# An RWKV-7 scan on one core: the output's store moved two thirds into the next period, a fourth buffer of V, and the second half's token tiles fetched one by one

## The chip, the cores and the metric

One core of a Trainium2 chip runs the whole program. The metric is the device time of one execution in microseconds (us). Three runs of the kernel before gave 2653.22, 2655.47 and 2659.98 us; the median, 2655.47 us, is the number that the change is compared with. A fourth execution was profiled, and all rows below come from it.

## What is computed

The reference is a trunk of two layers on 1024 tokens of width 1024, in float32. The change lies in the second layer's mixer, RWKV-7 time mixing. Cut to what matters here:

```
r, k, v = projections of x;  w = decay(x);  a, g = gates(x)
kk = normalize(k * k_k);  k = k * (1 + (a - 1) * k_a)
per head of 64, over the tokens t in order:
    S = S * w_t + (S @ -kk_t) (kk_t * a_t)^T + v_t k_t^T
    y_t = S @ r_t
y = group_norm(y) * ln_g + ln_b + sum(r * k * r_k) * v
mix = (y * g) @ w_out                     # the output projection
x = LN(alpha * x + mix)                   # then the feed-forward block
```

## The kernel before

**The stages.** Layer 0 and its feed-forward block come first, then phase C (the projections of layer 1, written to scratch tensors in DRAM), phase D (the scan), phase E (the output projection with its layer norm) and the last feed-forward block. The change touches D and E.

**The scan (`phase_d`).** The scan works in 32 units: 16 chunks of 64 tokens times 2 groups of 8 heads. A unit passes through five generators: `cumulate` (E), `decay` (D), `scores` (P), `inverse` (I) and `chain` (C). One turn of the loop is called a period. In period i the chain of unit i runs beside the inverse of unit i+1, the scores of unit i+2, the decay of unit i+3 and the cumulated sum of unit i+4; the string `ORDER` says in which turn the generators take their steps. Tokens flow through the chain alone (C): it computes `z`, `p1`, `r1`, `py`, `UV`, `pS` and at last the output y, which TensorE leaves in `py` and which GpSimd (POOL) then normalizes, gains, adds to and gates in six operations (L1415, L1419 to L1421, L1424, L1431). Only after L1431 is y ready to be stored.

**The loads and stores of the scan.** All of them are issued on the queue of SyncE (SP), which works in order: an entry that waits for a semaphore holds every entry behind it. A period has 13 issues: two stores of y (L1446, the two halves of `store`), two loads each of V into `V` (L1236) and into `UV` (L1235), one each of SW and KN (L1219), four of K and KA (L1223) and one of R (L1225). Buffers are rings: `y` has 2, `V` 3, `R` 3, `UV` 4, and the tiles that take SW with KN and K with KA come from a pool of 8, which is four units' worth. V's buffer is free again once POOL has run L1423 (`bo`, the bonus) of the unit that held it; the tile of SW and KN is free once VectorE (DVE) has run L1271 of `decay`.

**What sets the order.** The program's text gives priorities, and a planner at build time puts every instruction into its engine's queue: among those that it takes to be ready by its own estimate, the earliest in the text comes first. So loads and early steps of later units run ahead of their place in the text, as far as the rings let them. `pace` adds an edge that the planner alone sees: the instruction gets its place in the queue not before the last matmul traced so far has its own; at run time it waits for nothing more. Before the change, `store(us[i - 1])` is the first thing in the text of period i, ahead of the loads, and it is not paced.

**The output projection (`phase_e`).** The 1024 tokens are 8 tiles (tt). For each tile `get_y` loads 128 rows of y (L1514 through L177, one of three `wraw` buffers) and the residual (L1518), lets POOL apply gain and bias to the residual (`ln_gain`, L355 and L356), turns y round on TensorE (L1525) and splits it into two parts on ScalarE (ACT) and DVE (L200, L203). `mmh(tt, n)` is a half of the projection: 24 matmuls (L232 to L234) against the weights `units[n]`, four tiles each of `w_o[n]`, which `load_unit` loads (L177, also `wraw`) and splits (L192 on ACT, L193 on DVE). `ln(tt)` is the layer norm with its reciprocal root on POOL (L272), its scaling on ACT (L279) and its transposes on TensorE (L298). Tiles 0 and 1 are done inside the end of the scan (`early`). Then the text has: the four loads of `w_o[1]`; tiles 2 and 3 (`get_y`, first half); `get_y` of tiles 4 to 7 in one go; the second half of tiles 0 to 3 with their layer norms; then the second half and after it the first half of tiles 4 to 7 with theirs.

Of the kernel before, what the change touches and what calls it, by code (L numbers as in the profile page):

```python
# [58 lines left out]
def f(ap):  # L59
    return ap.bitcast(F32)  # L60
# [13 lines left out]
AHEAD = 4  # L74
INV = 1

ORDER = "ICIPCEIPDICPIECDICPICICPDICI"
SCAN_EARLY = 32


E_EARLY, E_LOAD, E_TURN, E_PER, E_LN = 2, (175, 153, 140, 29), 33, 1, 1
# [66 lines left out]
def big(c, name, dtype=F32, cols=1024):  # L148

    t = c.pool.tile([P, SLOT * 4 // mybir.dt.size(dtype)], dtype, name=name, tag="big", bufs=N_ARENA)  # L150
    return t[:, 0:cols]


def tmp(c, name, dtype=F32):
    return c.pool.tile([P, 512], dtype, name=name, tag="t", bufs=N_T)
# [19 lines left out]
def raw_load(c, src, n=1024):  # L175
    raw = c.pool.tile([P, 1024], F32, name="wraw", tag="wraw", bufs=N_RAW)
    d = c.nc.sync.dma_start(raw[:, 0:n], src)  # L177
    if c.first_loads:
        after(c, d, c.first_loads)
    return raw  # L180


def load_unit(c, src, arena=False, lo_eng=None):

    nc = c.nc
    raw = raw_load(c, src)
    if arena:
        hi, lo = big(c, "whi", F32R), big(c, "wlo", F32R)
    else:
        hi = c.pool.tile([P, 1024], F32R, name="whi", tag="w", bufs=N_W)  # L190
        lo = c.pool.tile([P, 1024], F32R, name="wlo", tag="w", bufs=N_W)
    nc.scalar.copy(hi, raw)  # L192
    (lo_eng or nc.vector).tensor_tensor(lo, raw, f(hi), op=ALU.subtract)  # L193
    return hi, lo
# [11 lines left out]
def pace(c, ins):  # L206

    return after(c, ins, c.last_mm)


def after(c, ins, dep):

    c.tc.add_manual_dep(ins.ins, dep.ins.name, mybir.DependencyInfo(
        mybir.DependencyClass.NoSync, mybir.DependencyReason.SCHED_ONLY), reason="pace")
    return ins
# [932 lines left out]
def phase_d(c, scr, scrv, scry, l_g2):  # L1148
# [10 lines left out]
    nc, tc, sc = c.nc, c.tc, c.scan  # L1159
    NG = NH // 2 // HP  # L1160
    W = HP * CH
# [4 lines left out]
    half = [slice(0, 64), slice(64, 128)]  # L1166
# [3 lines left out]
    def rings(plan, n, dtype=F32):  # L1170
        pool, at = Ring(c, plan[0][0], n, sum(k for _, k in plan), dtype).bufs, 0
        for name, k in plan:
            r = Ring.__new__(Ring)
            r.bufs, r.i = pool[at:at + k], 0
            at += k
            R1[name] = r
    rings([("ra", INV + 3), ("bk", 2), ("bktm", NA), ("UV", INV + 3), ("AT", 2 * NA)], 2 * W)
    rings([("R", 3), ("cl", 2), ("Em", 2), ("rk", 2), ("S", 2 * NG), ("dS", 2), ("u1", 2), ("y", 2),
           ("V", 3), ("gg", 2), ("bo", 2)], W)
    rings([("E", 4)], HP * (CH + 2))  # L1180
    rings([("TT", 2)], HP * P, F32R)
    rings([("zr", 3)], W, F32R)
# [3 lines left out]
    for i, t_ in enumerate(R1["AT"].bufs):  # L1186
        e = 1 - i % 2
# [5 lines left out]
    S = [None] * NG  # L1193
# [241 lines left out]
    seq = [(ch, g) for ch in range(T // CH) for g in range(NG)]  # L1435
    us = {}
# [5 lines left out]
    def store(u):  # L1442
        dst = scry[u.ch * CH:(u.ch + 1) * CH, u.g * 2 * W:(u.g + 1) * 2 * W].rearrange(
            "t (k e j) -> t e k j", k=HP, e=2)
        for e in range(2):
            nc.sync.dma_start(dst[:, e], u.y[half[e]])  # L1446

    def by_half(name):

# [11 lines left out]
    through(decay(us[0]))  # L1461
    for i in range(-INV - 1, len(seq)):
        gens = {}
        if i > 0:
            store(us[i - 1])
        if i + AHEAD + 1 < len(seq):
            load(i + AHEAD + 1, *seq[i + AHEAD + 1])
        if 0 <= i + INV + 1 < len(seq):
            load_v(us[i + INV + 1])
        if i + AHEAD < len(seq):  # L1470
            gens["E"] = cumulate(us[i + AHEAD])
        if i + INV + 2 < len(seq):
            gens["D"] = decay(us[i + INV + 2])
        if i >= 0:
            gens["C"] = chain(us[i], us.get(i + NG))
        if 0 <= i + INV < len(seq):
            gens["I"] = inverse(us[i + INV])
        if i + INV + 1 < len(seq):
            gens["P"] = scores(us[i + INV + 1])
        if i == 0:  # L1480
            g2 = c.pool.tile([P, 1024], F32, name="g2", tag="w", bufs=N_W)
            nc.sync.dma_start(g2, l_g2)
            g2 = g2.rearrange("p (g k e j) -> p g e k j", g=NG, k=HP, e=2)
            lg, lb = by_half("rln_g"), by_half("rln_b")
        for s in ORDER:
            if s in gens:
                fresh[0] = True
                next(gens[s], None)
                if s in "CIP":
                    yield  # L1490
        for gen in gens.values():
            assert next(gen, "end") == "end"
    store(us[len(seq) - 1])

def phase_e(c, scry, xres, w_o, scan, res):

    nc = c.nc  # L1500
    acc, xc, ys, st = [None] * 8, Seven(), [None] * 8, [None] * 8

    def last_unit():

        raw, r = raw_load(c, w_o[0, 3]), ([], [])
        for e in range(2):
            src = raw[:, e * 512:(e + 1) * 512]
            for lst, nm in zip(r, ("hi", "lo")):
                lst.append(tmp(c, "wq" + nm, F32R))
            split(c, r[0][e], r[1][e], src)  # L1510
        return r

    def get_y(tt, b):
        y = raw_load(c, scry[tt * P:(tt + 1) * P, :])  # L1514
        yh = big(c, "yh", F32R).rearrange("p (k t) -> p k t", k=KT)
        yl = big(c, "yl", F32R).rearrange("p (k t) -> p k t", k=KT)
        acc[tt] = big(c, "acc")
        nc.sync.dma_start(acc[tt], xres[tt * P:(tt + 1) * P, :])  # L1518
        ln_gain(c, acc[tt], rows_)
        st[tt] = norm_stats(c, D)  # L1520
        for q in range(2):
            pt = bank(c, b, "pt", [P, 4, P])
            for j in range(4):
                k = q * 4 + j
                c.last_mm = nc.tensor.transpose(pt[:, j, :], y[:, k * P:(k + 1) * P], c.ident)  # L1525
            split(c, yh[:, q * 4:q * 4 + 4, :], yl[:, q * 4:q * 4 + 4, :], pt)
            yield
        ys[tt] = yh, yl

    def mmh(tt, n, b):  # L1530
        p = bank(c, b, "po")
        for k in range(KT):
            mm3(c, p, ys[tt], units[n][k // 2], k == 0, k == KT - 1, lambda y_: y_[:, k, :],
                lambda w: w[k % 2] if isinstance(w, list) else w[:, (k % 2) * 512:(k % 2) * 512 + 512])
            yield
        an = acc[tt][:, n * 512:(n + 1) * 512]
        nc.vector.scalar_tensor_tensor(an, an, ALPHA, p, op0=ALU.mult, op1=ALU.add)
        nc.vector.bn_stats(st[tt][:, n, :], an)

    def ln(tt):  # L1540
        ln_to_T(c, acc[tt], tt, "mix1", xc, res, st=st[tt])

    def early():
        for tt in range(E_EARLY):
            if tt == 0:
                yield from get_y(tt, "c")
            if tt + 1 < E_EARLY:
                yield from get_y(tt + 1, "c")
            yield from mmh(tt, 0, "c")

    def through(gen):
        for _ in gen:
            pass
    total = 32 * sum(ORDER.count(s) for s in "CIP") - SCAN_EARLY
    rows_ = [big(c, "g_row"), c.pool.tile([P, 1024], F32, name="b_row", tag="w", bufs=N_W)]
    for r, n in zip(rows_, ("ffn0_g", "ffn0_b")):
        nc.sync.dma_start(r, c.row(n).to_broadcast([P, D]))
    units, first, i = [[], []], early(), 0
    for i in range(total):
        next(scan)  # L1560
        left = total - 1 - i
        for q in range(4):
            if left == E_LOAD[q]:
                units[0].append(load_unit(c, w_o[0, q]) if q < 3 else last_unit())
        if left < E_TURN:
            for _ in range(E_PER):
                next(first, None)
    assert next(scan, "end") == "end"
    through(first)
    units[0][3] = load_unit(c, w_o[0, 3])  # L1570
    units[1] = [load_unit(c, w_o[1, q], arena=True) for q in range(4)]
    done = E_EARLY
    for h in range(2):
        for tt in range(4 * h, 4 * h + 4):
            if ys[tt] is None:
                through(get_y(tt, "b"))
            if tt >= done:
                through(mmh(tt, h, "a"))
        if h == 0:
            for tt in range(4, 8):  # L1580
                through(get_y(tt, "b"))
        for tt in range(4 * h, 4 * h + 4):
            through(mmh(tt, 1 - h, "a"))
            if tt % 4 >= E_LN:
                ln(tt - E_LN)
        for tt in range(4 * h + 4 - E_LN, 4 * h + 4):
            ln(tt)
    return xc


# [77 lines left out]
```

## Time and profile before

| | |
|---|---|
| median of 3 runs | 2655.47 us (2653.22 to 2659.98) |
| the profiled execution: time | 2657.45 us |
| the profiled execution: span from first to last instruction | 2655.7 us |
| mean granted TensorE clock | 0.971 |
| TensorE (PE) busy | 2517.7 us, 95% |
| DVE, ACT, POOL busy | 1697.4, 1136.5, 517.8 us |

The span is 1.75 us shorter than the execution's own time, and that time is 1.98 us over the median. Busy shares are means over stages of different kinds. The scan's periods lie between 1380 and 1860 us of the span, the rest of phase E up to about 1952 us. In the rows, PE is TensorE's matmuls, a trailing q marks an engine's queue, and the granted clock is a share of the full 2.4 GHz; the chip grants either 1.2 or 2.4 GHz, so a mean between 0.5 and 1.0 is a mixture of both.

### The profile page before, as it was taken

What the parts mean: (1) busy time and instruction counts of PE and PEld (TensorE: products, weight loads), DVE (VectorE), ACT (ScalarE), POOL (GpSimd) and SP (SyncE); (2) the same over time, 40 slices, a digit from 0 to 9 for tenths busy, and PEclk for the clock granted to TensorE, in tenths of its full rate; (3) what the DMA queues carried; (4) which work ended last, traced back from release to release, by engine and by line L of the source; (5) the groups of instructions that cost most, each with busy time, mean ns of one, the idle gap of its engine ahead of it and who ended that gap; (6) DMA issues with size and microseconds to landing.
All of it is one profiled execution on the core that took longest, in us unless ns stands there. A gap on an engine that the chain in (4) does not pass through costs nothing.

```text
span 2655.7 us, 41419 instructions
## 1 busy us (share of the span) xinstructions
PE 2517.7 (95%) x16064; PEld 2004.7 (75%) x16064; DVE 1697.4 (64%) x2981; ACT 1136.5 (43%) x2192; POOL 517.8 (19%) x526
## 2 busy tenths in 40 slices
PE   8999999999999999999998878788899999999997
PEld 6677868888878786777777767676677888878785
DVE  7775596666648428777846667675477666657534
ACT  3115552323323327777746666674352333322230
POOL 0012250000007000010214555465300000006003
PEclk9999999999999999999998789899899999999999
DMA  3403322222235433555764333322223222225451
GB/s 145 125 20 109 115 84 88 87 80 80 81 126 198 150 124 107 163 157 165 207 164 101 91 89 86 76 52 96 105 88 103 80 87 74 86 99 188 146 169 64
DMA packets 257605, 295.79 MB, mean 111 GB/s; under 512 B 149888, under 2 KB 190976, under 8 KB 257408
## 3 DMA queue, kind: packets, MB, share of 16 engines
q1 hardware_dynamic: 256256, 291.05, 35.3%
q8 instruction: 126, 2.06, 0.3%
q10 hardware_dynamic: 1152, 2.10, 0.2%
q14 instruction: 71, 0.58, 0.1%
HBM read 219.56 MB, written 69.21 MB: 109 GB/s over the span
## 4 chain that ended last, share of the span: by engine, by line
PE 65%; DVE 9%; issue 9%; DMA 7%; POOL 6%; ACT 4%; SPq 1%; DVEq 0%; ACTq 0%; POOLq 0%
PE py L646 14%; PE pz L646 9%; PE px L646 8%; DMA wraw<-in_f_out_dram 2%; PE pv L232 2%; PE pd L232 1%; PE pd L233 1%; PE pd L234 1%; PE po L232 1%; PE po L233 1%; PE po L234 1%; PE pv L233 1%; POOL acc L355 1%; PE pv L234 1%; PE pA L1204 1%
## 5 line engine op out<-in xcount | busy, mean ns | idle before, releaser
L646 PE MATMUL py<-xch,wb 128*128 128x512 f32 x1056 | 356.5, 400 | 2.9 <-DVE u L695 2.1
L200 ACT CAST wb<-wraw 128x512 fp32r<-128x512 f32 x220 | 135.6, 619 | 398.6 <-PE py L646 177.4
L232 PE MATMUL pd<-wb,hh 128*128 128x512 f32 x704 | 277.5, 394 | 5.1 <-DVE acc L735 5.0
L234 PE MATMUL pd<-wb,hl 128*128 128x512 f32 x704 | 278.0, 395 | 0.0
L233 PE MATMUL pd<-wb,hh 128*128 128x512 f32 x704 | 277.7, 394 | 0.0
L646 PEld LDWEIGHTS py<-xch,wb 128*128 128x128 f32 x1056 | 199.7, 189 | 61.4 <-DVE u L695 15.3
L203 DVE TENSOR_TENSOR wb<-wraw,wb 128x512 fp32r<-128x512 f32 x220 | 171.8, 784 | 112.9 <-ACT wb L200 110.6
L355 POOL TENSOR_TENSOR acc<-acc,g_row 128x1024 f32<-128x1024 f32 x24 | 65.8, 2743 | 897.6 <-DMA acc<-res 880.3
L646 PE MATMUL px<-xch,wb 128*128 128x512 f32 x704 | 234.4, 396 | 3.3 <-ACT p L657 3.3
L646 PE MATMUL pz<-xch,wb 128*128 128x512 f32 x704 | 233.1, 392 | 4.5 <-ACT xch L200 4.5
L200 ACT CAST wb<-sums 128x512 fp32r<-128x512 f32 x176 | 108.8, 622 | 256.7 <-PE pz L646 145.2
L646 PE MATMUL py<-xcl,wb 128*128 128x512 f32 x528 | 209.0, 396 | 1.6 <-DVE xcl L203 1.6
L203 DVE TENSOR_TENSOR wb<-sums,wb 128x512 fp32r<-128x512 f32 x176 | 123.0, 702 | 102.6 <-ACT wb L200 101.7
L203 DVE TENSOR_TENSOR hl<-wraw,hh 128x1024 fp32r<-128x1024 f32 x72 | 126.9, 1771 | 89.5 <-ACT hh L200 89.4
L1204 PEld LDWEIGHTS <-lt 128*128 128x128 f16 x1792 | 88.0, 102 | 103.2 <-issue 77.7
L232 PEld LDWEIGHTS pd<-wb,hh 128*128 128x128 f32 x704 | 133.1, 189 | 37.3 <-issue 4.4
L646 PEld LDWEIGHTS px<-xch,wb 128*128 128x128 f32 x704 | 132.7, 189 | 35.2 <-ACT p L657 5.5
L646 PEld LDWEIGHTS pz<-xch,wb 128*128 128x128 f32 x704 | 132.0, 188 | 35.0 <-ACT xch L200 5.3
L1204 PE MATMUL pX<-lt 128*128 128x64 f16 x1280 | 92.2, 201 | 69.2 <-DVE lt L1337 38.8
L233 PEld LDWEIGHTS pd<-wb,hh 128*128 128x128 f32 x704 | 132.7, 189 | 30.0
L234 PEld LDWEIGHTS pd<-wb,hl 128*128 128x128 f32 x704 | 132.7, 189 | 29.7
L193 DVE TENSOR_TENSOR wlo<-wraw,whi 128x1024 fp32r<-128x1024 f32 x82 | 103.0, 1262 | 69.9 <-ACT whi L192 46.8
(313 smaller groups left out, 5706.6 us busy)
## 6 DMA issues: line engine op xcount, KB each, us to landing
wraw<-in_f_in_dram SPq DMA_DIRECT2D x96, 512.0 KB, 3.6
wraw<-scr_h SPq DMA_DIRECT2D x72, 512.0 KB, 3.9
scr_h<-hf SPq DMA_DIRECT2D x44, 512.0 KB, 2.6
wraw<-in_f_out_dram SPq DMA_DIRECT2D x88, 256.0 KB, 2.7
res<-acc SPq DMA_DIRECT2D x16, 512.0 KB, 2.6
acc<-res SPq DMA_DIRECT2D x16, 512.0 KB, 4.2
wraw<-in_w_r_dram SPq DMA_DIRECT2D x16, 512.0 KB, 4.0
wraw<-in_w_k_dram SPq DMA_DIRECT2D x16, 512.0 KB, 4.2
```

The costliest lines, as they stand in the source:

```text
L193: (lo_eng or nc.vector).tensor_tensor(lo, raw, f(hi), op=ALU.subtract)
L200: nc.scalar.copy(hi, src)
L203: return (eng or nc.vector).tensor_tensor(lo, src, f(hi), op=ALU.subtract)
L232: nc.tensor.matmul(ps, ls(ah), rs(bh), start=start, stop=False)
L233: nc.tensor.matmul(ps, ls(ah), rs(bl), start=False, stop=False)
L234: c.last_mm = nc.tensor.matmul(ps, ls(al), rs(bh), start=False, stop=stop)
L355: c.nc.gpsimd.tensor_tensor(x, x, rows[0], op=ALU.mult)
L646: c.last_mm = nc.tensor.matmul(ps, a_[:, k * P:(k + 1) * P], b_[:, k % 2, :], start=start and k == i == 0, stop=False, skip_group_check=True)
L1204: keep(nc.tensor.matmul(*a, **k))
```

## The change

In the scan the store becomes a generator of its own, Y. `ORDER` gets one Y after its twentieth letter, between the fifth and the sixth step of the chain, and both halves of the store are paced there. `store` of unit i-1 so stands in the text of period i behind its loads and behind two thirds of its steps. The ring of y grows from 2 to 3 and that of V from 3 to 4; together the rings of that size were 26 and become 28 pieces of 256 columns, four to a slot, so they still fill seven slots. In phase E the loads of `w_o[1]` come in pairs behind tile 2 and tile 3, `get_y` of tile tt+4 comes right behind the second half of tile tt, and the first half of tiles 4 to 7 comes before their second half.

```diff
-ORDER = "ICIPCEIPDICPIECDICPICICPDICI"
+ORDER = "ICIPCEIPDICPIECDICPIYCICPDICI"
...
-    rings([... ("u1", 2), ("y", 2),
-           ("V", 3), ("gg", 2), ("bo", 2)], W)
+    rings([... ("u1", 2), ("y", 3),
+           ("V", 4), ("gg", 2), ("bo", 2)], W)
...
         for e in range(2):
-            nc.sync.dma_start(dst[:, e], u.y[half[e]])
+            pace(c, nc.sync.dma_start(dst[:, e], u.y[half[e]]))
+        yield
...
     for i in range(-INV - 1, len(seq)):
         gens = {}
-        if i > 0:
-            store(us[i - 1])
...
             gens["P"] = scores(us[i + INV + 1])
+        if i > 0:
+            gens["Y"] = store(us[i - 1])
...
-    store(us[len(seq) - 1])
+    through(store(us[len(seq) - 1]))
...
     units[0][3] = load_unit(c, w_o[0, 3])
-    units[1] = [load_unit(c, w_o[1, q], arena=True) for q in range(4)]
-    done = E_EARLY
+    for tt in range(E_EARLY, 4):
+        through(get_y(tt, "b"))
+        through(mmh(tt, 0, "a"))
+        for q in range(2 * tt - 4, 2 * tt - 2):
+            units[1].append(load_unit(c, w_o[1, q], arena=True))
     for h in range(2):
         for tt in range(4 * h, 4 * h + 4):
-            if ys[tt] is None:
-                through(get_y(tt, "b"))
-            if tt >= done:
-                through(mmh(tt, h, "a"))
-        if h == 0:
-            for tt in range(4, 8):
-                through(get_y(tt, "b"))
-        for tt in range(4 * h, 4 * h + 4):
-            through(mmh(tt, 1 - h, "a"))
+            through(mmh(tt, 1, "a"))
+            if h == 0:
+
+                through(get_y(tt + 4, "b"))
             if tt % 4 >= E_LN:
                 ln(tt - E_LN)
         for tt in range(4 * h + 4 - E_LN, 4 * h + 4):
             ln(tt)
+        if h == 0:
+            for tt in range(4, 8):
+                through(mmh(tt, 0, "a"))
```

## Rows read from the trace of the kernel before

**Rows 1.** The page's head: span and instructions.

```profile
span 2655.7 us, 41419 instructions
```

**Rows 2.** Windows by stage: stretch, its length, busy us (instructions), clock, DMA.

```profile
core 0: us, PE busy (x) PEld busy (x) DVE busy (x) ACT busy (x) POOL busy (x), PEclk, DMA share, GB/s
1421.80:1740.30 318.50, 263.92 (x4490) 225.65 (x4487) 217.83 (x641) 203.18 (x600) 170.47 (x222) 0.87 0.38 87
1800.20:1860.00 59.80, 51.69 (x543) 40.31 (x541) 29.99 (x69) 23.58 (x56) 36.97 (x32) 0.91 0.33 106
1860.00:1952.00 92.00, 80.43 (x371) 65.22 (x369) 40.85 (x90) 29.64 (x52) 23.58 (x15) 0.93 0.25 96
```

**Rows 3.** The same stretch with line L1369 alone, one instruction in each period.

```profile
1421.80:1740.30 318.50, 8.26 (x22) 0.87 0.38 87
1740.30:1800.20 59.90, 1.88 (x5) 1.00 0.18 43
```

**Rows 4.** Waits of the SP queue, 1421.8 to 1740.3: us, times, longest us.

```profile
SPq L1446 <- POOL R L1423: 92.2, 21, 6.7
```

**Rows 5.** Waits of the engines, 1421.8 to 1740.3: us, times, longest us.

```profile
PE pX L1204 <- DVE lt L1337: 36.1, 38, 5.4
DVE R L1242 <- DMA ld<-scr_SW: 29.3, 14, 4.0
...
DVE dv L1255 <- POOL R L1400: 2.6, 1, 2.6
DVE wlo L193 <- ACT whi L192: 2.5, 3, 1.1
```

**Rows 6.** Timeline of the SP queue, periods 19 and 20: start, us, issue.

```profile
1665.83 0.37 SPq L1219 DMA_DIRECT2D ld<-scr_SW  x1
...
1683.08 1.25 SPq L1446 DMA_DIRECT2D scr_y<-R  x2
1684.44 1.25 SPq L1236 DMA_DIRECT2D R<-scr_v  x2
1686.11 0.37 SPq L1219 DMA_DIRECT2D ld<-scr_SW  x1
```

**Rows 7.** Timeline of DVE, then of POOL, in the same two periods.

```profile
1671.36 1.21 DVE L1242 TENSOR_TENSOR_SCAN R<-rst,ld 128x256 f32<-128x256 f32 x1
...
1677.84 0.42 DVE L1271 TENSOR_TENSOR ra<-ld,E 128x256 f32<-128x256 f32 x1 [0.37 <-PE pz L1204]
...
1690.05 0.69 DVE L1242 TENSOR_TENSOR_SCAN R<-rst,ld 128x256 f32<-128x256 f32 x1 [4.01 <-DMA ld<-scr_SW]
...
1683.01 0.61 POOL L1423 TENSOR_TENSOR R<-R,bon 128x256 f32<-128x256 f32 x1
```

**Rows 8.** Windows of single periods, 19 to 22 and 24, columns as in Rows 2.

```profile
1666.00:1678.80 12.80, 11.44 (x213) 9.69 (x210) 9.65 (x29) 8.45 (x28) 6.71 (x10) 0.96 0.34 77
1678.80:1695.50 16.70, 11.85 (x204) 9.90 (x201) 9.79 (x29) 9.81 (x28) 8.03 (x12) 0.87 0.31 70
1695.50:1711.60 16.10, 15.43 (x215) 13.46 (x212) 10.04 (x29) 8.59 (x27) 6.74 (x10) 0.61 0.28 63
1711.60:1727.50 15.90, 11.77 (x204) 9.84 (x199) 9.86 (x29) 9.75 (x28) 7.96 (x12) 0.82 0.33 73
...
1740.30:1752.30 12.00, 10.51 (x210) 8.95 (x208) 9.43 (x28) 9.27 (x26) 7.08 (x11) 1.00 0.23 51
```

**Rows 9.** Timelines at the scan's end: SP, ACT, PE and POOL.

```profile
1824.89 1.25 SPq L1446 DMA_DIRECT2D scr_y<-R  x2
...
1830.44 1.04 ACT L192 CAST whi<-wraw 128x1024 fp32r<-128x1024 f32 x1 [9.79 <-DMA wraw<-in_w_o_dram]
...
1832.08 0.37 PE L1204 MATMUL pX<-lt 128*128 128x64 f16 x4 [6.16 <-ACT lt L1328]
...
1816.74 3.39 POOL L355 TENSOR_TENSOR acc<-acc,g_row 128x1024 f32<-128x1024 f32 x1
```

**Rows 10.** Timeline of PE in phase E after the scan, its two longest waits.

```profile
1867.37 1.06 PE L1525 MATMUL pt<-ident,wraw 128*128 128x128 f32 x8 [2.22 <-DMA wraw<-scr_y]
...
1886.61 1.97 PE L298 MATMUL pt<-ident,acc 128*128 128x128 f32 x8 [7.81 <-ACT acc L279]
```

More of the change, by code (lines that the diff above doesn't have):

```diff
@@ L1177, in phase_d @@
     rings([("ra", INV + 3), ("bk", 2), ("bktm", NA), ("UV", INV + 3), ("AT", 2 * NA)], 2 * W)
-    rings([("R", 3), ("cl", 2), ("Em", 2), ("rk", 2), ("S", 2 * NG), ("dS", 2), ("u1", 2), ("y", 2),
-           ("V", 3), ("gg", 2), ("bo", 2)], W)
+    rings([("R", 3), ("cl", 2), ("Em", 2), ("rk", 2), ("S", 2 * NG), ("dS", 2), ("u1", 2), ("y", 3),
+           ("V", 4), ("gg", 2), ("bo", 2)], W)
     rings([("E", 4)], HP * (CH + 2))
```

## The prediction

> **What bounds the kernel now.** The page's head gives the span [rows 1]; the change reaches two stretches of it, so I read those by windows first. The scan's middle, 22 periods from 1421.8 us on, takes 318.5 us [rows 2, 3]: 14.48 us a period. TensorE is busy in only 263.9 of them, and its granted clock is 0.87 on the mean, so part of the time runs at the 1.2 GHz level. The five periods behind it, where the last loads have been issued, take 59.9 us at 1.00 [rows 3]: 12.0 each, with the same chain, inverse and scores. So 2.5 us of each earlier period are no work of TensorE's.
>
> The list of waits says what they are. VectorE stood 29.3 us, 14 times, before L1242, the cumulated sum of a later unit, until that unit's SW had landed [rows 5]. VectorE is in order, so the masked copies of the inverse (L1337) queue behind it, and TensorE in its turn waits 36.1 us for L1337 [rows 5]. The queue of SP says why SW is late: the store stood 92.2 us in 21 waits for POOL [rows 4]. The row names L1423, but L1423 starts as L1431 ends, so this is y's own last operation.
>
> Two neighbouring periods show both cases. In period 19 SW is issued at 1665.83, ahead of the store, and its sum runs at 1671.36 with no wait [rows 6, 7]; the period takes 12.8 us at 0.96 [rows 8]. In period 20 SW's tile is free when L1271 ends, at 1677.84 + 0.42 = 1678.26; but SP stands at the store until 1683.08, then issues two stores and two loads of V, and SW goes at 1686.11, 7.85 us late [rows 6, 7]. VectorE waits 4.01 us for it, and the period takes 16.7 [rows 7, 8]. Period 21 has SW in front again and yet takes 16.1, at a clock of 0.61 [rows 8]: the stall before it is paid a second time, in slower matmuls.
>
> In phase E TensorE has work for nearly all of its time (80.4 of 92.0 us [rows 2]) and a few long holes. One of 6.16 us at 1832.08 is the scan's end: ACT waited 9.79 us for a tile of w_o whose load stood behind the store of 1824.89, and that store waited for POOL, which was busy with a residual tile from 1816.74 on [rows 9]. One of 7.81 us at 1886.61 is the first layer norm, whose reciprocal root stands on POOL behind the residuals of tiles 4 to 7. One of 2.22 us at 1867.37 is a wait for y [rows 10].
>
> **The store to Y.** No instruction is added: 64 stores, as many loads. The store leaves the head of each period, and what it held (SW, KN, R, K, KA, V) can go before it. At its new place, some 8 us into a period of 12.8, y of the unit before has been ready for about 4 us (in period 20 the store went 4.3 us after the period's start [rows 6, 8]), so I cost the wait there at nothing: the period's own matmuls hide it. Behind it queue loads whose data is used more than a period later; were y late, they would wait as SW does now. Where SW goes at once, the period is that of period 19: 22 x 12.8 = 281.6, which is 36.9 us less than 318.5. Not all of it is the store's: one wait of 2.6 us for POOL and three of 2.5 us together for weights [rows 5] come from phase E's early work, which stays. That leaves 31.8 us.
>
> The price has two bounds. Below stands nothing, if another entry holds SW as long as the store did. Above stand 22 periods of 12.0 us, 54.5 us less. I take 31.8, because a period with SW in front is what the trace shows when the queue does what the change asks, and its clock was 0.96 with all loads in flight.
>
> **The fourth V and the third y.** They add no instruction and no slot. V's load now belongs to a unit one further on, and so stands behind SW in the text; before, V came from an earlier period's text and went first [rows 6]. If V were still in front, SW would go when L1423 has ended (1683.62) and two loads of V are issued (1.25 us and some 0.1): at 1685.0 in place of 1686.11. Of a mean stall of 29.3 / 14 = 2.1 us that mends 1.1 at most. The third y covers the later store: its buffer is asked for again three periods on. With two buffers that store would still have had a period to land, so this part is worth nothing either way.
>
> **Phase E.** Same loads, same matmuls, another order. With the store of unit 29 behind five steps of its period, w_o's load no longer stands behind it, and the 6.16 us go. With the residuals of tiles 4 to 7 asked for one by one, the first layer norm's root stands behind two of them and not four, and TensorE has the second half of tile 1 and a transpose to do meanwhile; the 7.81 us go. The wait for y stays. Bounds: nothing, if other holes open, and 6.16 + 7.81 + 2.22 = 16.2. A loss is possible too: four `get_y` stand now one by one in TensorE's order, and each can wait 2.22 us [rows 10], 8.9 in all. I take 6.16 + 7.81 = 14.0, nearest to the holes whose causes the new order takes away.
>
> **The sum.** Against the profiled execution's own 2657.45 us: -31.8 - 14.0 = 2611.7. That execution was 1.98 over the median, so 2609.7; I say 2610.
>
> **The rivals.**
>
> *V or another load takes the store's place.* SP is in order, and the planner fills it by its own estimate of POOL. By that estimate V may be free before SW in every second period, as the store was; then SP stands before V until L1423 ends, 0.6 us after the store would have gone. For it: the order of the two alternates from period to period now [rows 6]. Against it: V now ranks behind SW whenever both are ready. Price: 14 stalls, each shorter by 0 (VectorE's sum is planned earlier too) to 1.1 us, so 0 to 15; I take 8. With phase E: 2657.45 - 8 - 14 - 2 = 2633. The Trainium skill, DMA: Bandwidth & Descriptors, section on the anatomy of one DMA, says that a semaphore wait happens on the issuing sequencer, before the transfer is handed over; by that rule the wait merely passes to the next entry that has one, and the trace agrees as far as the store of period 20 goes.
>
> *The clock stays up as well.* Period 21 lost 3.3 us with no stall of its own, at 0.61 [rows 8]. If no stall is left, all periods may run at 1.00, as the five at the end do: 12.0 each. Then 54.5 - 5.1 = 49.4, with phase E 63.4: 2592. For it: those five periods. Against it: period 19 still had 0.96, with loads that the five lack. The Trainium skill, TensorE: Matmul & The Clock Gate, section on what is actually happening, says that the slow clock is the default and activity lifts it; the trace agrees, 1.00 where no stall is and 0.61 right behind the longest.
>
> *Slower: SW is held in every period.* Today 8 of 22 periods have SW in front. If V, now the first to be ready, stands in front of SW in all of them, no period can recover its clock: 20 to 22 in a row show that, 16.7, 16.1 and 15.9, mean 16.2 [rows 8]. 22 x 16.2 = 357, which is 38 us more; less 14 in phase E it gives 2680. It decides from a mean period of 14.48 + 14 / 22 = 15.1 us on. Against it stands V's lower rank.
>
> *No change.* The stall passes to other loads in as many periods as now, and phase E opens as many holes as it closes: 2655.
>
> **How the numbers follow.** My forecast has a chance of 0.48, V in the store's place 0.24, the full clock 0.13, no change 0.08, slower 0.07. The likeliest time is 2610. The range runs from the full clock with phase E at its upper bound (2592 - 2 = 2590) to V in the store's place with phase E at nothing (2633 + 14 = 2647); 0.15 is left out. 0.3%, about what a measurement of this kernel can tell from no change, is 8 us. Faster by more holds the first three cases, 0.85; the same 0.08; slower 0.07.
>
> **What would show it.** Right: L1446 waits a few us in all on SP's queue and stands two thirds into the period; L1242's wait for SW falls from 29.3 us to below 8; the 22 periods take 276 to 290 us with a clock of 0.93 or more; the waits of 6.16 and 7.81 us in phase E are gone. V in the store's place: L1236 waits for POOL on SP's queue, with SW behind it, and L1242 still waits 15 us or more. Wrong altogether: periods of 15 us and more throughout, or new waits of TensorE for y between the second halves of tiles 0 to 3.

## The result, and the profile after

| | before | after |
|---|---|---|
| median (4 runs each) | 2654.34 us | 2593.12 us (2591.67 to 2594.03) |
| ratio | | 0.9765, 95% interval 0.975 to 0.978 |
| span of the profiled execution | 2655.7 us | 2590.0 us |
| mean granted clock | 0.971 | 0.987 |

The kernel is 61 us faster; the forecast was 2610, some 44 us faster. Both terms of the sum were too small.

The scan's 22 periods are now the stretch from 1418.1 to 1700.1 us. In the first row below it took 282.0 us (318.5 in [rows 2]); the five periods behind it take 59.9 as before. Then come two periods of the steady kind, and four that are not (5, 6, 8 and 11). Columns as in the windows ahead of the prediction: length, busy time of each engine, granted clock, DMA share, GB/s.

```profile
1418.10:1700.10 282.00, 245.17 (x4491) 210.29 (x4490) 222.01 (x641) 202.38 (x600) 174.09 (x222) 0.95 0.43 98
1637.80:1650.30 12.50, 10.82 (x207) 9.20 (x206) 10.00 (x30) 9.11 (x29) 7.71 (x11) 1.00 0.40 86
1650.30:1662.70 12.40, 10.74 (x206) 9.12 (x206) 9.94 (x29) 9.04 (x28) 7.61 (x11) 1.00 0.40 86
1454.20:1469.50 15.30, 13.18 (x208) 11.49 (x206) 11.27 (x31) 10.26 (x30) 8.67 (x11) 0.78 0.45 110
1469.50:1483.40 13.90, 11.83 (x206) 10.26 (x206) 10.77 (x31) 10.25 (x30) 8.58 (x12) 0.88 0.35 77
1495.50:1510.60 15.10, 13.08 (x206) 11.44 (x206) 11.39 (x30) 9.98 (x29) 8.52 (x11) 0.77 0.43 104
1536.40:1551.70 15.30, 14.04 (x208) 12.24 (x206) 11.16 (x33) 9.51 (x29) 9.37 (x13) 0.67 0.32 71
1700.10:1760.00 59.90, 52.46 (x1024) 45.26 (x1022) 42.28 (x129) 43.65 (x120) 36.20 (x50) 1.00 0.20 43
```

So the 282.0 us are made of two kinds of period: 18 that take 282.0 - 59.6 = 222.4 us together, 12.4 each on the mean, and the four rows with a lower clock, 59.6 together. The waits in the 22 periods, of SP's queue (first row), of VectorE and of TensorE (last row):

```profile
SPq L1236 <- POOL R L1423: 48.2, 21, 3.8
...
DVE ra L1286 <- PE pA L1204: 23.6, 19, 1.3
DVE lt L1337 <- PE pX L1204: 15.0, 20, 0.8
...
DVE wlo L193 <- ACT whi L192: 3.2, 3, 1.1
...
PE pX L1204 <- DVE lt L1337: 10.3, 32, 0.6
```

SP still stands still for POOL, 48.2 us in 21 waits, but before V's load (L1236) and no longer before the store. And the row that headed VectorE's list before, L1242 for SW [rows 5], is gone; TensorE's wait for L1337 has fallen from 36.1 us [rows 5] to 10.3. SP's queue in period 20 shows why:

```profile
1650.78 0.55 SPq L1219 DMA_DIRECT2D ld<-scr_SW  x1
1651.37 0.51 SPq L1219 DMA_DIRECT2D ld<-scr_KN  x1
1654.86 1.25 SPq L1236 DMA_DIRECT2D R<-scr_v  x2
1656.15 1.27 SPq L1446 DMA_DIRECT2D scr_y<-R  x2
1657.53 0.54 SPq L1225 DMA_DIRECT2D R<-scr_R  x1
...
1655.04 1.21 DVE L1242 TENSOR_TENSOR_SCAN R<-rst,ld 128x256 f32<-128x256 f32 x1
...
1653.54 0.72 POOL L1431 TENSOR_TENSOR R<-R 128x256 f32<-128x256 f32 x1
1654.22 0.61 POOL L1423 TENSOR_TENSOR R<-R,bon 128x256 f32<-128x256 f32 x1
```

SW and KN go half a microsecond into the period. Then SP stands until L1423 ends (1654.22 + 0.61 = 1654.83) and issues V and, with no wait of its own, the store: y was ready at 1653.54 + 0.72 = 1654.26. What stands behind the waiting V (store, R, later K) is not used soon: in all 22 periods the engines wait for a load of the scan once, for 0.2 us. L1242 runs 4.26 us after SW was issued, with no wait.

Phase E by windows: the scan's last period (before, then after), and the stretch from the chain's last start to the end of the first long wait of the feed-forward block (before, then after). Below them stand TensorE's waits in that stretch: two rows of before, then three of after. The one of 2.2 us (L646) ends the stretch and is the same in both kernels.

```profile
1817.00:1842.20 25.20, 18.71 (x182) 13.79 (x183) 10.43 (x24) 7.01 (x18) 13.16 (x7) 0.80 0.34 117
1842.20:1979.30 137.10, 122.07 (x604) 97.45 (x603) 74.58 (x149) 53.38 (x99) 39.16 (x30) 0.95 0.29 102
```

```profile
1776.60:1792.80 16.20, 15.87 (x182) 11.64 (x183) 6.75 (x21) 5.20 (x16) 10.01 (x7) 1.00 0.06 10
1792.80:1916.35 123.55, 118.40 (x603) 95.01 (x604) 84.29 (x153) 57.25 (x102) 40.10 (x30) 0.99 0.38 135
```

```profile
PE pt L298 <- ACT acc L279: 8.6, 4, 7.8
PE pt L1525 <- DMA wraw<-scr_y: 3.2, 2, 2.2
...
PE pz L646 <- ACT xch L200: 2.2, 1, 2.2
PE pz L1204 <- ACT R L1375: 1.0, 1, 1.0
...
PE pt L298 <- ACT acc L279: 0.6, 2, 0.3
```

Both holes are gone, and so are the waits for y, which the prediction left in. The 65.7 us between the spans are then: 36.5 in the 22 periods, 9.0 in the scan's last period, 13.55 behind it, 3.8 ahead of period 2 and 2.8 in the rest of the feed-forward block. The last two lie outside what was changed; the starts of period 2 in nine profiled kernels with this place of the store and four buffers of V lie between 1418.1 and 1423.0, so 3.8 is mostly what one execution differs from another.

### The profile page after: what moved, and what is told of

It is laid out like the page before. It is cut to its first block, busy times and chain, and to the rows that moved or that the text cites. A ratio compares the mean times of both kernels' runs of the same rounds, so it can differ in the third digit from the quotient of the medians.

```text
span 2590.0 us, 41379 instructions
## 1 busy us (share of the span) xinstructions
PE 2487.4 (96%) x16064; PEld 1981.5 (77%) x16064; DVE 1703.2 (66%) x2981; ACT 1135.7 (44%) x2192; POOL 519.0 (20%) x526
## 4 chain that ended last, share of the span: by engine, by line
PE 68%; DVE 10%; issue 9%; ACT 5%; DMA 5%; POOL 3%; SPq 0%; DVEq 0%; ACTq 0%; POOLq 0%
PE py L646 14%; PE pz L646 9%; PE px L646 8%; PE po L232 2%; DMA wraw<-in_f_out_dram 2%; PE po L233 2%; PE po L234 2%; PE pd L232 2%; PE pd L233 2%; PE pd L234 2%; PE pv L232 2%; PE pX L1204 1%; PE pv L233 1%; PE pA L1204 1%; PE pv L234 1%
## 5 line engine op out<-in xcount | busy, mean ns | idle before, releaser
L646 PE MATMUL py<-xch,wb 128*128 128x512 f32 x1056 | 355.7, 399 | 3.2 <-DVE u L695 2.8
L646 PEld LDWEIGHTS py<-xch,wb 128*128 128x128 f32 x1056 | 199.6, 189 | 61.9 <-DVE u L695 16.0
L355 POOL TENSOR_TENSOR acc<-acc,g_row 128x1024 f32<-128x1024 f32 x24 | 67.4, 2807 | 889.9 <-DMA acc<-res 882.4
L646 PE MATMUL px<-xch,wb 128*128 128x512 f32 x704 | 234.5, 396 | 3.2 <-ACT p L657 3.2
L646 PE MATMUL pz<-xch,wb 128*128 128x512 f32 x704 | 233.0, 392 | 4.5 <-ACT xch L200 4.5
L646 PE MATMUL py<-xcl,wb 128*128 128x512 f32 x528 | 208.6, 395 | 1.1 <-DVE xcl L203 0.9
L646 PEld LDWEIGHTS px<-xch,wb 128*128 128x128 f32 x704 | 132.9, 189 | 35.0 <-ACT p L657 4.7
L646 PEld LDWEIGHTS pz<-xch,wb 128*128 128x128 f32 x704 | 132.2, 188 | 34.4 <-ACT xch L200 5.3
L193 DVE TENSOR_TENSOR wlo<-wraw,whi 128x1024 fp32r<-128x1024 f32 x82 | 105.1, 1289 | 60.0 <-ACT whi L192 36.3
L646 PE MATMUL px<-xcl,wb 128*128 128x512 f32 x352 | 139.5, 396 | 0.0
```

What stands on the lines that cost most here:

```text
L355: c.nc.gpsimd.tensor_tensor(x, x, rows[0], op=ALU.mult)
L646: c.last_mm = nc.tensor.matmul(ps, a_[:, k * P:(k + 1) * P], b_[:, k % 2, :], start=start and k == i == 0, stop=False, skip_group_check=True)
```

## The experiments

**Each stage alone.** `scan_alone` keeps the old phase E, `e_alone` the old scan.

```diff
scan_alone, from the changed kernel:
-    for tt in range(E_EARLY, 4):
-        through(get_y(tt, "b"))
-        through(mmh(tt, 0, "a"))
...
+    units[1] = [load_unit(c, w_o[1, q], arena=True) for q in range(4)]
+    done = E_EARLY
...
e_alone, from the changed kernel:
-ORDER = "ICIPCEIPDICPIECDICPIYCICPDICI"
+ORDER = "ICIPCEIPDICPIECDICPICICPDICI"
...
+        if i > 0:
+            store(us[i - 1])
...
```

> The scan's part of the change (Y two thirds into the period, three y, four V) with phase E as before. From the two traces the scan's first 29 periods gave back some 40 us, period 30 8.9 and the rest of phase E 13.5. Theory (the hole of 6.16 us in period 30 is the store's): period 30 is mended here too, and only the rest of phase E is missing: 2593 + 13.5 = 2607 us. Rival (that hole belongs to the order of the w_o loads): it stays, 2593 + 22.4 = 2615 us, with ACT waiting some 10 us for w_o in period 30.

> Phase E's part of the change with the scan as before. Theory: the first layer norm no longer stands behind four residuals, but the store of unit 29 still stands before the loads of the scan's end: 2654 - 13.5 = 2641 us, and VectorE's wait for SW stays near 29 us. Rival (the w_o order mends period 30 as well): 2654 - 22.4 = 2632 us.

Measured: scan alone 2609.4 us, 0.9836 (0.9812 to 0.986); phase E alone 2626.07, 0.9893 (0.9868 to 0.9917); the kernel before beside them 2651.97. The gains are 42.6 and 25.9, 68.5 together, where both edits at once gave 61.2 (each against the kernel before as measured beside it). The scan's last period accounts for that: it takes 16.2 us in either kernel alone. Before, in [rows 9], ACT waits in it for a tile of w_o behind a store. SP's queue in the scan's change alone, and ACT in phase E's change alone, tell how each mends that:

```profile
1771.59 7.08 SPq L177 DMA_DIRECT2D wraw<-in_w_o_dram  x3
...
1786.31 1.25 SPq L1446 DMA_DIRECT2D scr_y<-R  x2
```

```profile
1813.15 0.37 ACT L1369 CAST zr<-pz 128x256 fp32r<-128x256 f32 x1 [1.49 <-PE pz L1204]
...
1829.37 0.38 ACT L1369 CAST zr<-pz 128x256 fp32r<-128x256 f32 x1
...
1830.32 1.05 ACT L192 CAST whi<-wraw 128x1024 fp32r<-128x1024 f32 x1
```

In the first, three tiles of w_o are issued well ahead of the store, which is now paced. In the second, the last period runs from L1369 at 1813.15 to the next L1369 at 1829.37, and the first cast of a tile of w_o (L192) comes behind it, so ACT no longer waits for one inside the period. Each edit takes away one side of the same wait, and 9.0 us can be won only once: 68.5 - 9.0 = 59.5. `scan_alone` came out as its theory had it. My expectation of `e_alone` gave this hole to the scan's store alone; its rival was right about the hole, and the time came out below the rival's 2632 as well.

**Three buffers of V, and four of them with the old store.**

```diff
v3, from the changed kernel:
-           ("V", 4), ("gg", 2), ("bo", 2)], W)
+           ("V", 3), ("gg", 2), ("bo", 2)], W)
v4_alone, from the kernel before:
-           ("V", 3), ("gg", 2), ("bo", 2)], W)
+           ("V", 4), ("gg", 2), ("bo", 2)], W)
```

> The changed kernel with three buffers of V, as before the change. Theory (the store at the head of the period held SW, and with the store gone V is free in time): no wait of VectorE for SW, 2590 to 2597 us. Rival (the fourth V is needed, since V in front of SW waits for POOL as the store did): waits of VectorE for SW of 15 us or more in all, 2605 to 2620 us.

> The kernel before with a fourth buffer of V and nothing else. SW now stands behind the store but ahead of V. Theory (the store holds SW): two issues of V, 1.35 us, less in front of SW in some 14 periods, so 0 to 19 us less than before: 2635 to 2654 us, and VectorE's wait for SW between 10 and 29 us. Rival (V was what held SW): no wait for SW, and the scan as in the changed kernel: 2613 us.

Measured: `v3` 2653.82 us, 0.9996 (0.998 to 1.0011); `v4_alone` 2666.95, 1.0046 (1.0027 to 1.0066). Both are misses: neither theory nor rival had the time. With phase E's gain in it, `v3` is no faster than before: its 22 periods take 337.7 us, longer than the 318.5 of before. Its queue at period 19, with POOL and VectorE; then its 22 periods by window, and the waits in them:

```profile
1685.78 1.23 SPq L1236 DMA_DIRECT2D R<-scr_v  x2
1687.11 0.55 SPq L1219 DMA_DIRECT2D ld<-scr_SW  x1
...
1685.14 0.61 POOL L1423 TENSOR_TENSOR R<-R,bon 128x256 f32<-128x256 f32 x1
...
1690.23 0.69 DVE L1242 TENSOR_TENSOR_SCAN R<-rst,ld 128x256 f32<-128x256 f32 x1 [2.65 <-DMA ld<-scr_SW]
```

```profile
1419.40:1757.10 337.70, 280.95 (x4484) 240.59 (x4484) 217.92 (x641) 203.93 (x601) 169.54 (x223) 0.80 0.36 82
```

```profile
SPq L1236 <- POOL R L1423: 105.7, 22, 7.3
...
DVE R L1242 <- DMA ld<-scr_SW: 33.9, 18, 4.2
```

V now stands directly in front of SW in every period and waits for L1423, and L1242 waits for SW 18 times. That is the mechanism of the prediction's slower rival, at 337.7 / 22 = 15.35 us a period in place of its 16.2. The fourth V is what puts V behind SW: the load then belongs to a unit one further on. `v4_alone` is the mirror image. Its V does go behind SW, and the store, unmoved, is all that is left in front:

```profile
1418.10:1748.40 330.30, 281.37 (x4492) 240.77 (x4490) 217.95 (x645) 203.96 (x600) 169.98 (x222) 0.80 0.36 84
```

```profile
SPq L1446 <- POOL R L1423: 103.0, 20, 10.1
...
DVE R L1242 <- DMA ld<-scr_SW: 29.5, 17, 3.1
```

The windows and the waits of its 22 periods are shown. The store waits 103.0 us, in 20 waits, and stands before SW in most periods. L1242 stands still no longer in all than before, 29.5 us against 29.3 in [rows 5], but its 14 stalls have become 17, and the clock is 0.80 against 0.87 in [rows 2]. So in the scan the fourth V alone costs 330.3 - 318.5 = 11.8 us, the store's new place without it 337.7 - 318.5 = 19.2, and both together win 36.5, each as one profiled execution shows it.

**Place, third y, and the order of phase E.** From the changed kernel:

```diff
y_head:
-ORDER = "ICIPCEIPDICPIECDICPIYCICPDICI"
+ORDER = "YICIPCEIPDICPIECDICPICICPDICI"
y2:
-    rings([... ("u1", 2), ("y", 3),
+    rings([... ("u1", 2), ("y", 2),
e_one:
+    units[1] = [load_unit(c, w_o[1, q], arena=True) for q in range(4)]
     for tt in range(E_EARLY, 4):
         through(get_y(tt, "b"))
         through(mmh(tt, 0, "a"))
-        for q in range(2 * tt - 4, 2 * tt - 2):
-            units[1].append(load_unit(c, w_o[1, q], arena=True))
```

> The changed kernel with the store's letter Y at the head of the period, still paced, with four V and three y. Theory (what the scan gains is where the store stands in SP's queue, and at the head it stands before SW and waits for POOL): L1446 waits on SP for 50 us or more in all, L1242 waits for SW in most periods, the scan as with four V alone, 2630 to 2650 us. Rival (the buffers or the pacing as such make the gain): 2590 to 2600.

> The changed kernel with two buffers of y in place of three. Theory (the third buffer is worth nothing, since a store two thirds into the period still has a period to land): 2590 to 2597 us, within 0.3% of the changed kernel, and no wait of TensorE or VectorE for a y buffer. Rival (the copy that fills y must wait for a store of the period before): a wait of some us in most periods, 2600 to 2630.

> The changed kernel with the four loads of the second half's weights in one go ahead of tiles 2 and 3, as before; tiles 4 to 7 still fetched one by one. It splits the 13.5 us that phase E is shorter behind the scan, of which the kernel with the scan's change alone shows none. Theory (the hole before the first layer norm, 7.81 us, and the clock lost behind it are the fetch in one go; the weights' order is worth a few us at most): 2594 to 2600. Rival (the weights in pairs keep ScalarE and the wraw buffers free and carry most of it): 2603 to 2609.

Measured: `y_head` 2636.96, 0.9941 (0.9919 to 0.9963); `y2` 2595.73, 0.9773 (0.9757 to 0.9789); `e_one` 2594.85, 0.9772 (0.9757 to 0.9787). All three as the theories had it. The 22 periods of `y_head`, with the waits of SP and VectorE in them:

```profile
1418.40:1744.50 326.10, 276.28 (x4490) 237.16 (x4490) 217.34 (x642) 203.28 (x600) 169.45 (x223) 0.83 0.38 85
...
SPq L1446 <- POOL R L1423: 103.3, 22, 6.1
...
DVE R L1242 <- DMA ld<-scr_SW: 26.2, 14, 3.8
```

With the buffers and the pacing in place but Y at the head, L1446 waits 103.3 us on SP, L1242 waits for SW 14 times, and the scan is slow again: it is the place in the queue that counts. Whether the new place would do without the pacing was not run. The third y is worth nothing that can be measured. And phase E splits: here is the stretch behind the scan with the old order (`scan_alone`), with its long waits, and with the new order of the tiles but the weights loaded in one go (`e_one`), where the first of these waits is down to 0.8 us and the second is gone:

```profile
1793.80:1930.10 136.30, 122.66 (x604) 98.12 (x604) 74.58 (x149) 53.53 (x99) 39.12 (x30) 0.95 0.30 103
```

```profile
PE pt L298 <- ACT acc L279: 7.0, 4, 6.2
PE pt L1526 <- DMA wraw<-scr_y: 2.9, 1, 2.9
```

```profile
1794.50:1915.90 121.40, 117.27 (x603) 94.32 (x603) 77.09 (x149) 53.40 (x99) 38.51 (x30) 1.00 0.34 115
```

14.9 us come from the new order of tiles 4 to 7, wait for y included, while loading the second half's weights in pairs gives nothing there (123.55 in the changed kernel). The new order is two edits, the fetch one by one and the first half of these tiles ahead of their second; they were not run apart.

**A version that beats both.** The four slow periods have a cause of their own: early work of phase E, which the planner pulls forward as far as the buffers let it. In three, VectorE waits 1.1 us for a cast of w_o (L192) and then subtracts for 1.6 (L193). In the fourth, POOL holds a residual tile. `spread` cuts three early tiles of w_o into quarters and paces each, and paces the first residual; `spread2` does the same to the fourth tile; `spread3` and `spread4` ask for that one 55 and 90 steps ahead of the scan's end, not 29. The loop below is that of a tile's quarters, one turn for each step of the scan; the last lines are those of `spread4`.

```diff
+    for e in range(9):
+        s = slice((e - 4) * 256, (e - 3) * 256)
+        if e >= 4 and e < 8:
+            pace(c, nc.scalar.copy(part(hi, e - 4), raw[:, s]))
+        s = slice((e - 5) * 256, (e - 4) * 256)
+        if e >= 5:
+            pace(c, nc.vector.tensor_tensor(part(lo, e - 5), raw[:, s], ...))
+        yield
...
-E_EARLY, E_LOAD, ... = 2, (175, 153, 140, 29), ...
+E_EARLY, E_LOAD, ... = 2, (175, 153, 140, 90), ...
```

> A version meant to beat the changed kernel: the three early tiles of w_o are split in quarters, each paced to its place in the text in the scan's last third, and the first residual tile is paced too, so that no 128x1024 operation of VectorE and none of POOL falls into the scan at once. Theory (periods 5, 6, 8 and 11 of the changed kernel are 3.2, 1.8, 3.1 and 3.2 us over their neighbours for these operations): about 11 us off, 2580 to 2587, these periods at 12.1 to 12.5 us and a clock of 1.00. Rival (the same work lands in the last periods and costs there what it cost before): 2590 to 2600.

> As the version spread, with the fourth early tile of w_o split in paced quarters too. In spread the four mended periods came back to 12.1 to 12.5 us, but its periods 26 and 27 took 17.0 and 16.3 where the changed kernel has 12.1 and 11.8, behind two 128x512 casts of ScalarE and two subtractions of VectorE for that tile. Theory (those splits are the cause): periods 26 and 27 below 13, about 9 us off, 2583 to 2588. Rival (the quarters only move the cost on, to the scan's last periods or behind it): 2591 to 2597.

> As spread2, with the fourth early tile of w_o asked for 55 steps ahead of the scan's end and not 29. In spread2 its last pieces came after the scan, TensorE waited 1.89 us for one, and periods 29 and 30 took 17.6 and 19.9 us where the changed kernel has 16.6 and 16.2. Theory (that is only lateness): periods 29 and 30 as in the changed kernel, 4 to 5 us off, 2581 to 2585. Rival (the pieces cost the same in the period they now fall into): 2586 to 2590.

> As spread3, with 90 steps, so that the pieces fall a period or two further ahead of the first tile of y. Theory and rival as for spread3: 2581 to 2585 or 2586 to 2590; if the two differ by more than 3 us, it matters which period the pieces fall into.

> The changed kernel once more, on the same chip as spread3 and spread4, as the measure for them. Both theories: its ratio to the kernel before is 0.975 to 0.978, as measured at first.

Measured: `spread` 2593.91, 0.977 (0.9755 to 0.9785), the rival's number: the four periods are mended, but the fourth tile, still whole, now hits period 26, which with 27 takes 33.3 us. `spread2` 2587.75, 0.9757 (0.974 to 0.9774), on the edge of the theory: those two are mended, but the pieces come so late that periods 29 and 30 take 17.6 and 19.9 us, where the changed kernel has 16.6 and 16.2. Then, on one chip: `spread3` 2588.6, 0.9757 (0.9743 to 0.9772); `spread4` 2585.62, 0.9748 (0.9732 to 0.9764); the changed kernel again 2595.84, 0.9784 (0.9769 to 0.9798), a little above what I expected of it. `spread3` mends period 30 (16.2) and loses most of that in period 29 (20.0); `spread4` lies between theory and rival, with the full clock in every period from the second on. Its 22 periods:

```profile
1420.50:1692.70 272.20, 236.27 (x4491) 201.66 (x4490) 216.28 (x641) 200.13 (x599) 166.60 (x220) 1.00 0.43 94
```

272.2 us at 1.00 throughout, 9.8 less than the change left, and `spread4` is 10.2 us faster than the changed kernel beside it; the two intervals do not touch. That shows what the early work cost.

## Why the prediction was right, step by step

*What bounds the scan* was right: SW behind the waiting store. `y_head`, `v3` and `v4_alone` each put something that waits for POOL back in front of SW, by three different edits, and each time the stalls of L1242 and the low clock came back. L1446 itself, 92.2 us in [rows 4], does not wait in the 22 periods of the changed kernel. It goes out 5.5 to 9.0 us into a period, 6.6 on the mean and behind V, where the forecast had some 8; y is ready 3.6 to 5.7 us into the period, so the wait that was costed at nothing is nothing.

*The store to Y: -31.8 forecast, -36.5 measured.* The mechanism held; two sizes were off and partly cancel. "Where SW goes at once, the period is that of period 19", 12.8 us, was too long: at a clock of 0.96 that period still paid for its neighbours. With no stall near, it is 12.4, as `spread4` shows for all 22 (272.2 / 22). That is 46.3 less than 318.5, not 36.9. And the waits of phase E's early work, costed at 5.1 by the length of the waits alone, cost 9.8: the subtraction itself and the clock lost behind it count too.

*The fourth V* was argued rightly (its rank is what puts it behind SW), but its weight was underrated: "mends 1.1 at most" is the price of a V in front as the kernel before had it, not of one in front in every period. Without it the scan is 19 us slower than before. *The third y* at nothing was right.

*Phase E: -14.0 forecast, -22.5 measured.* Both holes went. The first was sized by its idle time, 6.16; the period lost 9.0, since its matmuls ran at a mean clock of 0.80 (TensorE is busy 18.71 us in it before and 15.87 after). The second was 7.81 of 13.55. "The wait for y stays" was the step that failed: the two of them, 3.2 us, are gone, and `e_one` shows that the new order of the tiles does that too. The rest is again clock, 0.95 against 0.99: TensorE is busy 122.07 us there before and 118.40 after, for the same matmuls. A new wait of 1.0 us for L1375 takes a little back.

*The rivals.* The total, 2593, is that of the full clock (2592), but by another route: its price for the scan, 49.4, was too high by 13, and phase E, with the stretches outside, made up for it. Of the 13, 272.2 - 264 = 8.2 are the period itself, which in these 22 takes 12.4 us at the full clock and not the 12.0 of the five behind them; the rest is the early work, at 9.8 and not 5.1. Its mechanism is right in 18 periods of 22. V does take the store's place on SP, 48.2 us, yet holds nothing urgent, so that rival's price was nothing. The slower rival's mechanism is real and was one buffer away.

## What to carry to other kernels

On an in-order queue, ask for every entry that waits what stands behind it and when that is needed; a wait costs nothing when only late-needed entries follow. Moving one waiting entry and reordering the next can be worth nothing or a loss alone and a gain together, so read the whole order of the queue after the edit, not the entry that moved. Price a stall by the whole periods around it: here the matmuls behind it ran at a lower clock as well, 0.61 in [rows 8].

## What the runs showed of the hardware

Some operations of VectorE and POOL held each other up for whole instructions. Just behind the scan of the changed kernel, VectorE's subtraction (L193) meets POOL's residual (L355, L356); the first row is the same subtraction with POOL idle:

```profile
1800.10 1.23 DVE L193 TENSOR_TENSOR wlo<-wraw,whi 128x1024 fp32r<-128x1024 f32 x1
...
1807.83 6.29 DVE L193 TENSOR_TENSOR wlo<-wraw,whi 128x1024 fp32r<-128x1024 f32 x2
...
1807.29 2.41 POOL L355 TENSOR_TENSOR acc<-acc,g_row 128x1024 f32<-128x1024 f32 x1
1809.78 3.26 POOL L356 TENSOR_TENSOR acc<-acc,b_row 128x1024 f32<-128x1024 f32 x1
...
1534.99 2.21 DVE L1255 TENSOR_TENSOR dv<-dend,dmid 128x4 f32<-128x4 f32 x1
...
1534.78 2.41 POOL L356 TENSOR_TENSOR acc<-acc,b_row 128x1024 f32<-128x1024 f32 x1
```

Two subtractions of 1.2 us take 6.29 beside two of POOL's. Taken in turns, that is 1807.29 + 2.41 = 1809.70 for L355, 1.2 for the first subtraction, some 2.3 for L356 (which so seems to last 3.26), 1.2 for the second: 1814.4, where the second ends at 1807.83 + 6.29 = 1814.12. The early subtractions of the scan take 1.6 us in place of 1.2 in the same way: the one that starts at 1456.08 meets POOL's L1421, which ends at 1456.61, and ends 1.1 us behind that. In the last two rows a VectorE operation on 128x4, 0.13 us elsewhere, ends with POOL's L356 and seems to take 2.21: this is what disturbed period 11, which takes 12.5 us in `spread`, where that residual is paced. The Trainium skill, SBUF — State Buffer, section on the two separate sides, says that the two engines share a port pair under an exclusive lock, that a VectorE instruction with two inputs in SBUF comes under it against a POOL instruction that reads SBUF, and that whoever starts first keeps it for its whole instruction; these rows agree with it.

The clock also fell on slight occasion. In the changed kernel one wait of 1.1 us and a 1.6 us subtraction were followed by 0.77 and 0.78 in two periods and 0.88 in a third. TensorE's own waits in the first of them were 0.7 us at the longest. In the second profiled run of the same kernel that period kept 1.00 and took 13.4 us in place of 15.3, and the one behind it fell to 0.77.
